# An expert stage in 16 units of several blocks, with TensorE in written order and weights in 8 KB pairs

## The chip, the cores and the metric

The kernel runs on one core of a Trainium2 chip. The core has five engines that work side by side, each through its own list of instructions in order: TensorE (PE, matrix products; its weight loads are PEld), VectorE (DVE), ScalarE (ACT), GpSimd (POOL) and SyncE (SP). SP here only issues loads. Sixteen DMA engines move data between the chip's memory (HBM) and the on-chip memory (SBUF); TensorE writes its products into PSUM banks of 128 x 512 floats. The metric is the time of one launch in microseconds, the median of several runs.

## What is computed

One decoder block for 512 tokens of width 1024: a mixer (a Mamba-2 part and a short convolution), then a mixture of experts, each with a residual and a layer norm. The change concerns the mixture:

```python
def moe_ffn(h, router_w, router_bias, w_gate, w_up, w_down, sh_gate, sh_up, sh_down):
    ...
    _, e_idx = lax.top_k(jnp.where(expert_mask, biased, -jnp.inf), TOP_K)
    gate = jnp.take_along_axis(scores, e_idx, axis=1)
    gate = gate / jnp.sum(gate, axis=-1, keepdims=True) * ROUTED_SCALE
    ...
    def expert_block(args):
        xb, e = args
        return (jax.nn.silu(xb @ w_gate[e]) * (xb @ w_up[e])) @ w_down[e]
    ...
    routed = jax.ops.segment_sum(yb * row_gate[:, None], row_tok, num_segments=T + 1)[:T]
    shared = (jax.nn.silu(hf @ sh_gate) * (hf @ sh_up)) @ sh_down
    return (routed + shared).reshape(b, s, d)
```

There are 64 experts; each token goes to 8 of them. An expert has a gate and an up matrix of 1024 x 256 and a down matrix of 256 x 1024, 3.1 MB in float32. So 201 MB of weights are read by whatever tokens there are. All arithmetic is in float32.

## The kernel before

The first 800 us or so are the mixer, then come the output projection, the routing and the shared expert. The expert stage begins at 872 us. Two experts have their place fixed at build time (the "static" unit); the other 62 are ranked by their number of tokens, and the ranks are read into registers, so that each load takes its expert from a register.

**Blocks.** A block is 128 slots of tokens, gathered from memory by an indirect DMA on POOL (`slots`, line 1055). There are 41. In 13 of them all slots belong to one expert: these use `matmul3` (lines 124 to 127), three matmuls for one product, since weights and tokens are split into a high and a low part (`split`: ScalarE writes the high part, line 130, VectorE the rest, line 132). In the other 28 several experts share the block, 64 or 32 slots each: these use `tiled` (line 883), which for one step issues a matmul per expert, each on its own columns of the array, with unsplit float32 weights. A step is one of the 8 slices of 128 of the contraction in the up part, or one of 2 x 2 in the down part, so a tiled block has 12.

**Units.** `kinds` makes the units by letter: x is the heaviest expert with its partner (three blocks), y and z a heavy expert with a lighter one (a plain and a tiled block), f one full expert, a, p and q tiled blocks of two, two and four experts. `ORDER` has 31 letters; with the static unit that is 32 units. Every unit runs through `ffn` in stages: quarters 0 to 3 of gate and up, activation (`act_t`, with transposes), then down, whose results `expert` scales (line 1083) and splits. After every second finished block (`GRP`) `combine` puts rows back in token order by 16 matmuls for each block (lines 1106, 1107) and eight adds on VectorE (line 1112). The first quarter of the next unit is written ahead of this unit's down part. A scheduler orders every engine's instructions by when they can run, TensorE's too.

**Weights.** `piece` loads a quarter of gate and up (two DMAs of 256 KB, rows of 2 KB) or half of down (one of 512 KB, rows of 4 KB) into a page of 4 KB in each of the 128 partitions: ten DMAs for each expert. Pages come from a pool of 14 (`pages`), which the mixer uses too, and some from a second pool (`pb_`). `plan` writes down the loads in order, `take` issues them up to `AHEAD` pieces before they are used. All go through SP's one queue, and a load waits there until its page is free.

Of the kernel before, what the change touches and what calls it, by code (L numbers as in the profile page):

```python
# [26 lines left out]
NPAGB = 9  # L27
# [5 lines left out]
XA = 3  # L33
# [3 lines left out]
ORDER = "azqxqyyppaypayaaafazaaafafafpaz"  # L37
AHEAD = 14
# [3 lines left out]
BEY = 100  # L42
# [11 lines left out]
PSPLIT = (3,)  # L54
NPS = 0
SPB = ((0, 0, 0), (0, 1, 0), (0, 0, 1), (0, 1, 1), (0, 0, 2))
# [7 lines left out]
def block_kernel(ctx: ExitStack, tc: tile.TileContext, a, out, dbg=None):  # L64
# [9 lines left out]
    pa = ctx.enter_context(tc.tile_pool(name="pages", bufs=NPAGE))  # L74
# [15 lines left out]

    def page(shape, dt=F32, pool=None):
        n = 1
        for q in shape:
            n *= q
        assert n == 1024
        return (pool or pa).tile([P, *shape], dt, name="pg", tag="pg")
# [39 lines left out]
    def split(src, eng=None):  # L136
# [8 lines left out]
        elif len(src.shape) == 4:  # L145

            split_to(hi, lo, src.rearrange("p a b c -> p (a b c)"), eng)
            return tuple(t.rearrange("p (a b c) -> p a b c", a=src.shape[1], b=src.shape[2]) for t in (hi, lo))
# [134 lines left out]
    for k in range(KD):  # L283
        if k + 1 < KD:
            ada_mm(k + 1)
        for i, c0 in enumerate(first):
            if k == 0:
                if i < 3:
                    fw[i] = split(win.pop(c0))
                else:  # L290
                    fw[i] = (page([KD, P], FR), page([KD, P], FR))
# [76 lines left out]
    def ssd_proj(g):  # L368
        d = sst.setdefault(g, {})
        if g == 0:  # L370
# [3 lines left out]
            parts_ = page([KD, P], FR), page([KD, P], FR)  # L374
# [32 lines left out]
    def ssd_core(g):  # L407
# [97 lines left out]
        for i in range(2):  # L505
            tl = 2 * g + i
            if tl % 2 == 0:
                d0 = (page([2, T], FR), page([2, T], FR))
# [29 lines left out]
    def sc_conv(j):  # L538
# [18 lines left out]
        if j % 2 == 0:  # L557
            d0 = (page([2, T], FR), page([2, T], FR))
# [162 lines left out]
    sgb = [page([2, T]) for _ in range(4)]  # L721
# [21 lines left out]
    def wo_load():  # L743
# [3 lines left out]
        if j < 5:  # L747
            pool = pb_ if j < 2 else pa
            wo.append((page([D], FR, pool), page([D], FR, pool)))
# [87 lines left out]
    def piece(q, wg, wu, wd, pool=None):  # L837

        if q < 4:
# [8 lines left out]
    def xsplit(src_ap, dst=None, whole=False):  # L848
# [4 lines left out]
        for q in range(2):  # L853
            tp = bank("tr", 2)
            for k in range(4):
                transpose(tp[:, k * P:(k + 1) * P], sv[:, 4 * q + k, :])
            tv = tp.rearrange("p (k n) -> p k n", k=4)
            sl_ = slice(4 * q, 4 * q + 4)
            if whole:
                S.activation(hi[:, sl_, :], tv, AF.Copy)  # L860
            else:
                split_to(hi[:, sl_, :], lo[:, sl_, :], tv)
        return hi, lo

    def act_t(o, whole):
# [3 lines left out]
        V.tensor_tensor(sg, sg, o[:, FE:], op=OP.mult)  # L869
        tp = bank("tr", 2)  # L870
# [375 lines left out]
    for i, u in enumerate(units):  # L1246
        steps += [(u, j) for j in (1, 2, 3)]
        if i + 1 < len(units):
            steps.append((units[i + 1], 0))
# [176 lines left out]
```

## Time and profile before

| what | us |
|---|---|
| median of three runs | 1611.98 (1609.96 to 1613.97) |
| the profiled execution | 1601.06 |
| its span | 1599.3 |
| expert stage in it, first tiled matmul to last combine matmul | 712.2 (872.3 to 1584.5) |

The profile is one execution. Its time is 1.8 us more than its span. Everything below is read from this execution; the runs that were timed lie some 10 us above it. Lines of the trace name an operation by its source line, the tile it writes and the tiles it reads: `ps_pj<-pg,xt` is a product of a weight page and transposed tokens into a PSUM bank. `xN` counts records.

### The profile page before, as it was taken

What the parts mean: (1) busy time and instruction counts of PE and PEld (TensorE: products, weight loads), DVE (VectorE), ACT (ScalarE), POOL (GpSimd) and SP (SyncE); (2) the same over time, 40 slices, a digit from 0 to 9 for tenths busy, and PEclk for the clock granted to TensorE, in tenths of its full rate; (3) what the DMA queues carried; (4) which work ended last, traced back from release to release, by engine and by line L of the source; (5) the groups of instructions that cost most, each with busy time, mean ns of one, the idle gap of its engine ahead of it and who ended that gap; (6) DMA issues with size and microseconds to landing.
All of it is one profiled execution on the core that took longest, in us unless ns stands there. A gap on an engine that the chain in (4) does not pass through costs nothing. (4 is left out here: it accounts for less than half of the span.)

```text
span 1599.3 us, 24806 instructions
## 1 busy us (share of the span) xinstructions
PE 1525.1 (95%) x8253; PEld 1009.2 (63%) x8253; DVE 978.3 (61%) x1760; ACT 643.3 (40%) x926; POOL 312.5 (20%) x314
## 2 busy tenths in 40 slices
PE   6999899999999999999988899999999999999996
PEld 4688787787787877888765445454454445446643
DVE  5557778667868656536786354564464456447646
ACT  3556575555634545434441323142233123223323
POOL 0011111011001456400035121221111212111211
PEclk9999999999999999999989999999999999999998
DMA  9763333534340677626363989787999799899991
GB/s 277 178 166 94 101 78 80 147 84 101 105 116 17 195 222 223 174 79 199 151 211 100 289 280 367 268 311 212 343 322 315 247 365 334 245 333 328 360 316 66
DMA packets 240599, 335.82 MB, mean 210 GB/s; under 512 B 18548, under 2 KB 141780, under 8 KB 240468
## 3 DMA queue, kind: packets, MB, share of 16 engines
q1 hardware_dynamic: 229380, 303.75, 59.3%
q0 software_dynamic: 11088, 30.45, 7.0%
q8 instruction: 67, 1.10, 0.3%
q14 instruction: 64, 0.52, 0.1%
HBM read 334.58 MB, written 4.28 MB: 212 GB/s over the span
## 5 line engine op out<-in xcount | busy, mean ns | idle before, releaser
L132 DVE TENSOR_TENSOR wl<-pg,wh 128x1024 fp32r<-128x1024 f32 (+1 forms) x201 | 245.5, 1226 | 164.2 <-ACT wh L130 163.8
L130 ACT ACTIVATE wh<-pg 128x1024 fp32r<-128x1024 f32 (+1 forms) x207 | 202.2, 987 | 232.5 <-PE ps_pj L126 101.9
L125 PE MATMUL ps_pj<-hm,wh 128*128 128x512 f32 x680 | 274.6, 405 | 2.1 <-ACT wh L130 2.1
L127 PE MATMUL ps_pj<-hm,wl 128*128 128x512 f32 x680 | 267.0, 393 | 5.5 <-DVE wl L132 5.5
L126 PE MATMUL ps_pj<-hm,wh 128*128 128x512 f32 x680 | 266.4, 392 | 0.0
L887 PE MATMUL ps_pj<-pg,xt 128*32 128x512 f32 (+1 forms) x1472 | 247.7, 600 | 0.0
L125 PEld LDWEIGHTS ps_pj<-hm,wh 128*128 128x128 f32 x680 | 128.1, 188 | 36.2 <-issue 5.5
L127 PEld LDWEIGHTS ps_pj<-hm,wl 128*128 128x128 f32 x680 | 128.0, 188 | 35.5 <-DVE wl L132 8.3
L126 PEld LDWEIGHTS ps_pj<-hm,wh 128*128 128x128 f32 x680 | 128.0, 188 | 28.8 <-issue 3.4
L887 PEld LDWEIGHTS ps_pj<-pg,xt 128*32 128x32 f32 (+1 forms) x1472 | 63.4, 115 | 110.8 <-issue 101.8
L1112 DVE TENSOR_TENSOR res<-res,ps_y 128x512 f32<-128x512 f32 x152 | 102.6, 686 | 42.1 <-PE ps_y L1107 40.4
L1083 DVE SCALAR_TENSOR_TENSOR wk<-ps_y,red,pg 128x512 f32<-128x512 f32 x82 | 61.1, 748 | 88.1 <-PE ps_y L887 57.1
L1055 POOL DMA_INDIRECT pg<-h_d,idx x41 | 49.8, 1215 | 326.7 <-DVE oh L1039 78.5
L887 PE MATMUL ps_y<-pg,wkr 128*32 128x512 f32 (+1 forms) x736 | 107.5, 596 | 2.0 <-DMA pg<-in_w_down_dram 2.0
L1079 POOL TENSOR_SCALAR oht<-iota_t,tok 128x512 fp32r<-128x512 f32 x41 | 67.1, 1642 | 129.1 <-PE ps_y L1107 128.9
L1107 PE MATMUL ps_y<-pg,oht 128*128 128x512 f32 x224 | 89.4, 402 | 0.0
L338 POOL TENSOR_TENSOR pg<-pg 128x1024 f32<-128x1024 f32 x28 | 73.9, 2653 | 53.9 <-ACT pg L336 53.8
L868 ACT ACTIVATE sg<-ps_pj 128x256 f32<-128x256 f32 x44 | 16.9, 384 | 163.9 <-PE ps_pj L887 112.2
L122 PEld LDWEIGHTS ps_tr<-ident,pg 128*128 128x128 f32 x392 | 56.7, 191 | 34.4 <-ACT wkr L878 10.8
L125 PE MATMUL ps_pj<-pg,wh 128*128 128x512 f32 x192 | 75.0, 391 | 2.8 <-ACT zs L403 2.8
L127 PE MATMUL ps_pj<-pg,wl 128*128 128x512 f32 x192 | 75.3, 392 | 0.0
L122 PE MATMUL ps_tr<-ident,pg 128*128 128x128 f32 x392 | 68.6, 290 | 6.8 <-DMA pg<-h_d,idx 1.8
(383 smaller groups left out, 2550.9 us busy)
## 6 DMA issues: line engine op xcount, KB each, us to landing
pg<-in_w_gate_dram SPq DMA_DIRECT2D x256, 256.0 KB
pg<-in_w_up_dram SPq DMA_DIRECT2D x256, 256.0 KB
pg<-in_w_down_dram SPq DMA_DIRECT2D x128, 512.0 KB
pg<-in_w_in_dram SPq DMA_DIRECT2D x88, 512.0 KB
pg<-in_w_ada_dram SPq DMA_DIRECT2D x48, 512.0 KB
bc<-acs_d POOLq DMA_DIRECT2D x32, 256.0 KB, 5.2
pg<-in_w_ssd_out_dram SPq DMA_DIRECT2D x16, 512.0 KB
pg<-in_w_sc_out_dram SPq DMA_DIRECT2D x8, 512.0 KB
```

The costliest lines, as they stand in the source:

```text
L122: return PE.transpose(o, i, ident[:n, :n])
L125: PE.matmul(o, lh, rh, start=start, stop=False)
L126: PE.matmul(o, lh, rl, start=False, stop=False)
L127: PE.matmul(o, ll, rh, start=False, stop=stop)
L130: S.activation(hi, src, AF.Copy)
L132: V.tensor_tensor(lo, src, rw(hi), op=OP.subtract)
L338: GP.tensor_tensor(part[i], part[i], w, op=OP.add)
L887: PE.matmul(o[w * i:w * i + w, :], x[:, w * i:w * i + w], m, start=start, stop=stop, tile_position=(0, w * i))
L1079: GP.tensor_scalar(res_[b][0], iota_t, tok, None, op0=OP.is_equal)
L1083: V.scalar_tensor_tensor(yg, o, red[:, 1:2], g2b[:, ns_], op0=OP.mult, op1=OP.mult)
L1107: PE.matmul(o, oh_, yl[:, ns_], start=False, stop=(i == len(parts) - 1))
L1112: V.tensor_tensor(ra[t][:, ns_], ra[t][:, ns_], o, op=OP.add)
```

## The change

- **Units.** 32 units become 16: the static one, and 15 words of letters. The blocks of all letters of a word form one unit, so that a unit has one to three blocks and two to six experts.
- **Order in a unit.** All its blocks go through quarter 0, then through quarter 1 in reverse order, and so on. Then follow the activations with two steps or more of the combine of the unit before between them, the transposes of the next unit's tokens, and the down part. `csteps` takes all finished blocks of the unit before at once, up to three where it was two before.
- **TensorE in written order.** From the second unit on, TensorE's instructions stand as the program writes them (`tc.manual_schedule`); the other engines are still ordered by the scheduler.
- **Memory.** The pool of single pages ends after the shared expert's loads; a pool of seven pairs of 8 KB is opened in its place, taken in the fixed order `PORD`. One more pair comes from `pb_` for every eighth piece, so eight pairs rotate.
- **Loads.** A piece is half of gate and up (two DMAs of 512 KB, rows of 4 KB) or the whole of down (one of 1 MB, rows of 8 KB): five DMAs for each expert. `AHEAD` is 10 pieces.
- **The count of overflowing tokens** (`beyond`) is cut in three steps and put between others.

```diff
--- before.py
+++ after.py
@@ -24,22 +24,25 @@
 NPAGE = 14
-NPAGB = 9
+NPAIR = 7
+
+PORD = (4, 6, 3, 5, 1, 0, 2)
+NPAGB = 5
+NPAPB = 2
...
 GRP = 2
-XA = 3
+MAN = 1
 NXG = 3
...
-ORDER = "azqxqyyppaypayaaafazaaafafafpaz"
-AHEAD = 14
+ORDER = "x qy ya ap za qff ya ap za faa ya ap za faa p"
+AHEAD = 10
...
@@ -71,7 +71,9 @@
-    pa = ctx.enter_context(tc.tile_pool(name="pages", bufs=NPAGE))
+
+    pa_cm = tc.tile_pool(name="pages", bufs=NPAGE, side="right")
+    pa, pw = pa_cm.__enter__(), []
@@ -88,12 +90,38 @@
+    def pair(shape, dt=F32, pool=None):
...
+        if pool:
+            return pool.tile([P, *shape], dt, name="pr", tag="pr", bufs=NPAPB)
+        npr[0] += 1
+        return pw[0].tile([P, *shape], dt, name="pr", tag="pr%d" % PORD[npr[0] % NPAIR])
...
@@ -836,37 +863,73 @@
     def piece(q, wg, wu, wd, pool=None):
 
+        if q < 2:
+            r = pair([2, 4, FE], pool=pool)
+            for i, w in enumerate((wg, wu)):
+                SY.dma_start(r[:, i], w.rearrange("(p k) n -> p k n", k=KD)[:, 4 * q:4 * q + 4, :])
+        else:
+            r = pair([2, D], pool=pool)
+            SY.dma_start(r, wd.rearrange("(p k) n -> p k n", k=2))
+        return r
...
         if q < 4:
-            r = page([2, 2, FE], pool=pool)
+            r = page([2, 2, FE])
             for i, w in enumerate((wg, wu)):
                 SY.dma_start(r[:, i], w.rearrange("(p k) n -> p k n", k=KD)[:, 2 * q:2 * q + 2, :])
         else:
-            r = page([D], pool=pool)
+            r = page([D])
             SY.dma_start(r, wd.rearrange("(p k) n -> p k n", k=2)[:, q - 4, :])
         return r
...
@@ -887,27 +950,33 @@
-            for o, (xh, xl), b in zip(os_, xs, blocks):
+            for o, (xh, xl), b in list(zip(os_, xs, blocks))[::-1 if q % 2 else 1]:
                 for k in (2 * q, 2 * q + 1):
...
             if q == 3:
-                acts = [act_t(o, len(b) > 1) for o, b in zip(os_, blocks)]
+                sgs = [act_in(o) for o in os_]
             yield
+        acts = []
+        for sg, b in zip(sgs, blocks):
+            acts.append(act_t(sg, len(b) > 1))
+            yield
+        yield
...
@@ -1087,30 +1161,34 @@
             if n == 1:
                 parts.append(res_[b])
-                if len(parts) == GRP and not tail[0]:
-                    combine()
...
-    def combine(last=False):
-
+    def csteps(last=False):
+
+        ps_ = list(parts)
+        parts.clear()
         for t in range(NT):
...
@@ -1131,8 +1209,13 @@
-    shw = [piece(q, a["sh_gate"][0], a["sh_up"][0], a["sh_down"][0]) for q in range(6)]
-    ring = [lambda: (page([D], FR, pb_), page([D], FR, pb_)),
+    shw = [page_piece(q, a["sh_gate"][0], a["sh_up"][0], a["sh_down"][0]) for q in range(6)]
+    pa_cm.__exit__(None, None, None)
+    pw.append(ctx.enter_context(tc.tile_pool(name="pairs", bufs=1, side="right", reuse_waits="tile")))
+    for i in range(NPAIR):
+
+        pw[0].tile([P, 2048], F32, name="pl", tag="pr%d" % i)
+    ring = [lambda: two([D], FR, pb_),
             lambda: (rww.rearrange("p k i e -> p (k i e)"), page([D], FR, pb_)), lambda: (hm[6], hm[7])]
...
@@ -1239,39 +1321,44 @@
-    units += [kinds[k].pop(0) for k in ORDER.replace(" ", "")]
+    for ks in ORDER.split():
+
+        rs, bl = (), []
+        for k in ks:
+            r_, b_ = kinds[k].pop(0)
+            bl += [(tuple(len(rs) + e for e in es), sl_) for es, sl_ in b_]
+            rs += r_
+        units.append((rs, bl))
...
@@ -1303,25 +1392,42 @@
+    def unit(n):
...
+        need_x(i1)
+        run = expert([b for b, _ in units[n][1]], sl[i0:i1], xs[i0:i1], lambda e, q: take((n, e, q), AHEAD))
+        for _ in range(4):
+            next(run)
+        com = csteps() if parts else iter(())
+        for _ in range(2):
+            next(com, None)
+        for _ in range(i1 - i0):
+            next(run)
+            next(com, None)
+        zipper(xs_steps(i2), com, islice(over_, 1))
+        next(run)
+        tail[0] = n + 1 == len(units)
+        drain(run)
...
-    running, i1 = {}, 0
-    for i, (u, j) in enumerate(steps):
-        if j == 0:
-            i0 = ublk[id(u)]
-            i1 = i0 + len(u[1])
-            need_x(i1)
-            running[id(u)] = expert([b for b, _ in u[1]], sl[i0:i1], xs[i0:i1],
-                                    lambda e, q, n=unum[id(u)]: take((n, e, q), AHEAD),
-                                    PSPLIT if unum[id(u)] < NPS else ())
-        if i + XA < len(steps) and steps[i + XA][1] == 0 and len(xs) == i1:
-            need_x(i1 + 1)
...
-        next(running[id(u)], None)
-    combine(True)
+    for n in range(MAN):
+        unit(n)
+    over_ = beyond()
+
+    with tc.manual_schedule(engines={mybir.EngineType.PE}):
+        for n in range(MAN, len(units)):
+            unit(n)
+        combine(True)
+    ostart, oend, obase, nov = far
```

Three things are the same: the number of TensorE instructions, that of gathers, and the order of TensorE, VectorE and ScalarE up to the expert stage. VectorE has 32 fewer adds.

TensorE before, in a unit with one plain and one tiled block of two experts, first and second quarter (L887 is a tiled matmul, L125 to L127 are the three of `matmul3`, `ps_pj` the banks of the up part, `pg` a weight page):

```order
L125 MATMUL ps_pj<-wh_80,xt 128x512
L126 MATMUL ps_pj<-wl_81,xt 128x512
L127 MATMUL ps_pj<-wh_80,xt 128x512
L887 MATMUL ps_pj<-pg,xt 64x512 x3
L125 MATMUL ps_pj<-wh_76,xt 128x512
L887 MATMUL ps_pj<-pg,xt 64x512
L126 MATMUL ps_pj<-wl_77,xt 128x512
L127 MATMUL ps_pj<-wh_76,xt 128x512
```

Of the four tiled matmuls that make two steps, three stand together and the fourth is apart, behind a plain one: the second step is cut.

TensorE after, in a unit with a plain block, a tiled block of two experts and one of four (`ya`; lines moved: L950 is `tiled`, L153 to L155 `matmul3`, `pr` a pair), from the end of the down part before it to the second quarter:

```order
L950 MATMUL ps_y<-pr,wkr 64x512 x8
L153 MATMUL ps_pj<-wh_76,xt 128x512
L154 MATMUL ps_pj<-wl_77,xt 128x512
L155 MATMUL ps_pj<-wh_76,xt 128x512
L153 MATMUL ps_pj<-wh_76,xt 128x512
L154 MATMUL ps_pj<-wl_77,xt 128x512
L155 MATMUL ps_pj<-wh_76,xt 128x512
L950 MATMUL ps_pj<-pr,xt 64x512 x4
L950 MATMUL ps_pj<-pr,xt 32x512 x16
L950 MATMUL ps_pj<-pr,xt 64x512 x4
L153 MATMUL ps_pj<-wh_78,xt 128x512
```

The tiled blocks of quarter 0 and quarter 1 stand in one row, 4 + 16 + 4 matmuls, with nothing between them, and the plain block's matmuls stand ahead and behind.

SP before, loads of gate and up pages and of down pages (a register and an ISA row ahead of each load fetch the expert's number):

```order
L842 DMA pg<-in_w_up_dram 128x512
L842 REGISTER_ALU
L842 ISA
L842 DMA pg<-in_w_gate_dram 128x512
L842 REGISTER_ALU
L842 ISA
L842 DMA pg<-in_w_up_dram 128x512
L845 REGISTER_ALU x2
L845 ISA
L845 DMA pg<-in_w_down_dram 128x1024
L845 REGISTER_ALU x2
L845 ISA
```

SP after, at the same kind of place:

```order
L869 DMA pr<-in_w_up_dram 128x1024
L869 REGISTER_ALU x2
L869 ISA
L869 DMA pr<-in_w_gate_dram 128x1024
L869 REGISTER_ALU x2
L869 ISA
L869 DMA pr<-in_w_up_dram 128x1024
L872 REGISTER_ALU x2
L872 ISA
L872 DMA pr<-in_w_down_dram 128x2048
L872 REGISTER_ALU x2
L872 ISA
```

Where there was a load of 128 x 512 floats for a quarter and 128 x 1024 for half of down, there is now one of 128 x 1024 for a half of gate or up and one of 128 x 2048 for the whole of down.

## Rows read from the trace of the kernel before

**Rows 1.** The head of the page

```profile
span 1599.3 us, 24806 instructions
```

**Rows 2.** Windows, the expert stage: us, busy us (instructions) per engine, clock, DMA share, GB/s

```profile
872.30:1584.50 712.20, 696.40 (x4152) 354.15 (x4150) 379.83 (x648) 205.47 (x328) 131.86 (x123) 1.00 0.87 295
```

**Rows 3.** Waits of TensorE in the stage: us, times, longest

```profile
PE ps_y L1106 <- ACT rww L130: 2.7, 2, 2.2
```

**Rows 4.** Groups by form in the stage: shapes xcount, busy us, mean ns, idle before

```profile
L887 PE MATMUL ps_pj<-pg,xt 128*32 128x512 f32 x1152 | 156.7, 597 | 0.0
L1112 DVE TENSOR_TENSOR res<-res,ps_y 128x512 f32<-128x512 f32 x152 | 102.6, 686 | 42.1 <-PE ps_y L1107 40.4 <-issue 1.1
L887 PE MATMUL ps_pj<-pg,xt 128*64 128x512 f32 x320 | 91.3, 612 | 0.0
...
L132 DVE TENSOR_TENSOR wl<-pg,wh 128x1024 fp32r<-128x1024 f32 x72 | 88.5, 1233 | 51.1 <-ACT wh L130 51.0
L130 ACT ACTIVATE wh<-pg 128x1024 fp32r<-128x1024 f32 x72 | 75.0, 1054 | 102.6 <-DMA pg<-in_w_up_dram 41.9 <-DMA pg<-in_w_down_dram 27.7 <-PE ps_pj L127 22.9
L887 PE MATMUL ps_y<-pg,wkr 128*32 128x512 f32 x576 | 71.0, 596 | 2.0 <-DMA pg<-in_w_down_dram 2.0
...
L887 PE MATMUL ps_y<-pg,wkr 128*64 128x512 f32 x160 | 36.5, 598 | 0.0
```

**Rows 5.** Timeline of TensorE: start, us, line, out<-in, xcount

```profile
999.51 1.05 PE L887 MATMUL ps_pj<-pg,xt 128*32 128x512 f32 x2
1000.48 0.50 PE L1106 MATMUL ps_y<-rww,oht 128*128 128x512 f32 x1
...
1002.30 1.05 PE L887 MATMUL ps_pj<-pg,xt 128*32 128x512 f32 x2
1003.27 0.50 PE L1107 MATMUL ps_y<-hm,oht 128*128 128x512 f32 x1
```

**Rows 6.** Timeline of TensorE, two other places

```profile
1014.61 3.65 PE L887 MATMUL ps_y<-pg,wkr 128*64 128x512 f32 x16
1018.20 0.50 PE L1106 MATMUL ps_y<-pg,oht 128*128 128x512 f32 x1
...
1330.74 1.06 PE L887 MATMUL ps_pj<-pg,xt 128*32 128x512 f32 x8
1331.74 0.51 PE L1107 MATMUL ps_y<-pg,oht 128*128 128x512 f32 x1
1332.08 0.39 PE L1106 MATMUL ps_y<-pg,oht 128*128 128x512 f32 x1
1332.32 0.39 PE L1107 MATMUL ps_y<-pg,oht 128*128 128x512 f32 x1
```

**Rows 7.** DMA queue in 6 us (961, 1027, 937, 973): packets, MB, share

```profile
q1 hardware_dynamic: 627, 2.27, 99.5%
...
q1 hardware_dynamic: 683, 2.49, 102.2%
...
q1 hardware_dynamic: 1072, 1.95, 98.7%
...
q1 hardware_dynamic: 1163, 2.12, 101.9%
```

**Rows 8.** DMA issues in the stage: count, median us to landing

```profile
pg<-h_d,idx POOLq DMA_INDIRECT x40, 8.2
```

**Rows 9.** Waits of SP's queue, 880 to 1560: us, times, longest

```profile
SPq L842 <- PE ps_pj L887: 65.2, 32, 9.4
...
SPq L845 <- PE ps_y L887: 40.7, 18, 12.0
```

**Rows 10.** Timeline of TensorE, and a window's row at the clock's fall

```profile
882.60 1.18 PE L122 MATMUL ps_tr<-ident,pg 128*128 128x128 f32 x8 [1.85 <-DMA pg<-h_d,idx]
883.72 5.39 PE L887 MATMUL ps_pj<-pg,xt 128*64 128x512 f32 x16
...
883.70:887.10 3.40, 3.40 (x7) 0.76 (x6) 0.00 (x0) 0.73 (x2) 0.21 (x1) 0.51 0.83 301
```

More of the change, by code (lines that the diff above doesn't have):

```diff
@@ L41 @@
 NADA = 3
-BEY = 100
 ENG3 = ("PP", "VV", "VV", "VV")
@@ L95, in page, with two @@
         assert n == 1024
-        return (pool or pa).tile([P, *shape], dt, name="pg", tag="pg")
+        if pool or not pw:
+            return (pool or pa).tile([P, *shape], dt, name="pg", tag="pg")
+        if not halves:
+            t = pair([2, 1024], dt)
+            halves.extend((t[:, 1], t[:, 0]))
+        return halves.pop()
+    def two(shape, dt=F32, pool=None):
+        if pool:
+            t = pair([2, *shape], dt, pool)
+            return t[:, 0], t[:, 1]
+        return page(shape, dt), page(shape, dt)
     def wk():
@@ L557, in sc_conv @@
         if j % 2 == 0:
-            d0 = (page([2, T], FR), page([2, T], FR))
+            d0 = two([2, T], FR)
             for q in range(2):
@@ L718, in block_kernel @@
         next(ada, None)
-    sgb = [page([2, T]) for _ in range(4)]
+    sgb = [h for _ in range(2) for h in two([2, T])]
     for j in range(KD):
@@ L747, in wo_load @@
         if j < 5:
-            pool = pb_ if j < 2 else pa
-            wo.append((page([D], FR, pool), page([D], FR, pool)))
+            wo.append(two([D], FR, pb_ if j < 2 else None))
             split_to(*wo[j], r)
@@ L852, in xsplit, with steps, act_in @@
         sv = src_ap.rearrange("p (d k) -> p k d", k=KD)
[L853 to L865, printed above, removed]
+        def steps():
+            for q in range(2):
+                tp = bank("tr", 2)
+                for k in range(4):
+                    transpose(tp[:, k * P:(k + 1) * P], sv[:, 4 * q + k, :])
+                tv = tp.rearrange("p (k n) -> p k n", k=4)
+                sl_ = slice(4 * q, 4 * q + 4)
+                if whole:
+                    S.activation(hi[:, sl_, :], tv, AF.Copy)
+                else:
+                    split_to(hi[:, sl_, :], lo[:, sl_, :], tv)
+                yield
+        return (hi, lo), steps()
+    def xsplit(src_ap, dst=None, whole=False):
+        r, g = xsteps(src_ap, dst, whole)
+        for _ in g:
+            pass
+        return r
+    def act_in(o):
         sg = rt.tile([P, FE], F32, name="sg", bufs=2)
@@ L1058, in slots, with expert_piece, expert @@
         return xg, red
-    def expert_piece(sel_, q, pool=None):
-        return piece(q, *(a[nm][0, sel_].rearrange("o d f -> (o d) f") for nm in ("w_gate", "w_up", "w_down")), pool)
+    npc = [0]
+    def expert_piece(sel_, q):
+        npc[0] += 1
+        return piece(q, *(a[nm][0, sel_].rearrange("o d f -> (o d) f") for nm in ("w_gate", "w_up", "w_down")),
+                     None if npc[0] % (NPAIR + 1) != 3 else pb_)
     npart, tail = [0], [False]
-    def expert(blocks, sl_, xs, w, gp=()):
+    def expert(blocks, sl_, xs, w):
         res_ = []
@@ L1112, in combine @@
                     V.tensor_tensor(ra[t][:, ns_], ra[t][:, ns_], o, op=OP.add)
-        parts.clear()
+                yield
+    def combine(last=False):
+        for _ in csteps(last):
+            pass
     out_proj(0)
```

97 lines of the change are left out of this document (56 added, 41 removed).

## The prediction, made before the change was run

> **What bounds the kernel now.** I read the head of the page first [rows 1], then the busy time by stretch [rows 2], TensorE's waits [rows 3] and the instruction groups of the expert stage [rows 4]. The change touches nothing before the first tiled matmul (872.3 us) but the order of some loads, so only the stage from there to the last combine matmul (1584.5 us) matters: 712.2 us of the 1599.3 us span. In it TensorE is busy 696.4 us, the DMA engines 87% [rows 2]. TensorE is idle only 15.8 us there, and the list of what its matmuls waited for has nothing above 2.7 us [rows 3]. VectorE and ScalarE work half the time or less. So what would shorten the stage is less TensorE time, and DMA is the next thing in line: 0.87 x 712 = 620 us busy.
>
> But not all TensorE time is matrix work. Two prices show it.
> - A **run of tiled matmuls** (line 887) costs more than its steps. One step of a block (all its tiles, 8 records for four tiles) between two combine matmuls holds TensorE from 1330.74 to 1331.74, 1.00 us; the plain matmul behind it takes 0.34 instead of the 0.23 of its neighbours. Four steps in one run last 1014.61 to 1018.20, 3.59 us [rows 6]. With about 0.1 us lost at each end, one step and its ends are 1.20 us, four are 3.79; the difference gives 0.86 us a step and about 0.34 us for each run.
> - A **step that is cut** pays again. Two records of a four-tile step, a quarter of it, take 0.97 us before the next kind of matmul, and so does the next quarter [rows 5]: the four tiles work side by side, so a piece takes as long as the whole. Each cut costs another 0.86 us.
>
> 28 of the 41 blocks are tiled, 12 steps each, 336 steps: 289 us. The four L887 groups of TensorE add up to 156.7 + 91.3 + 71.0 + 36.5 = 355.5 us [rows 4], 66 us more. The scheduler that orders TensorE by readiness makes 133 tiled runs out of them with 42 extra passes for cut steps (counted in the order of instructions, of which two places stand above): 133 x 0.34 = 45 and 42 x 0.86 = 36 us. That is 81 us; records overlap and some fall on waits, so the agreement is rough but the excess is there.
>
> **What the change removes.** TensorE in program order from the second unit on, with the blocks of a unit reversed on odd quarters so that tiled blocks meet: 47 runs and 3 extra passes. Saved: 86 x 0.34 = 29 us and 39 x 0.86 = 33.5 us, **62.5 us** on the path. The number of matmuls is the same. 32 fewer adds on VectorE (152 x 686 ns before, [rows 4]) save 22 us of an engine that doesn't bound: nothing.
>
> **What it changes in the loads.** Rows of 2 KB for gate and up become 4 KB, of 4 KB for down 8 KB; a quarter of an expert's ten DMAs becomes half of five. Before has both sizes side by side: in 6 us stretches with only 4 KB rows the DMA queue moves 2.27 MB at 99.5% of the engines' time and 2.49 at 102.2%, so 380 and 406 GB/s; with only 2 KB rows 1.95 MB at 98.7% and 2.12 at 101.9%, 329 and 347 GB/s [rows 7]. A pair of 1.05 MB is then 2.76 us at 380, and 3.10 at 338 if size doesn't matter. I take 2.76, as the first is the row with the new size. With 64 x 3 pairs and 41 gathers (0.52 MB each, so 1.4 us at the same rate) the loads need 530 + 57 = 587 us, against 620 now. Issuing is off the path: SP mostly waits for buffers, 65.2 us for one reader alone [rows 9].
>
> The Trainium skill ("DMA: Bandwidth & Descriptors", Specifications) puts the HBM limit of one core at about 358 GB/s, which speaks against a gain from longer rows. By it a pair would take an estimated 2.93 us and the loads 620 us. The trace passes that limit at 380 and 406 GB/s [rows 7], so I stay with the measured rate.
>
> **What it adds: waits.** Eight pairs rotate (seven of the pool and one of the hold), in fixed order, and a pair is read by all blocks of a unit, so that a unit's first-half pairs come free only when TensorE has done its first two quarters. Piece j waits for the release of piece j-8, at the head of SP's queue, with all later loads behind it.
> - Units of six experts (qy, qff): two of six second-half pairs are there, four must come after the release: 1.1 us to start and 4 x 2.76 = 12.1 us. TensorE has one tiled block's two steps (1.7 us) and a plain block's six matmuls (1.4 us) to do in between: 9 us idle, twice, 18 us.
> - Units of five (faa, twice): two must come, 6.6 us less 3.1 us: 3.5 us, twice, 7 us.
> - Units of four fit in eight pairs. The three ap have two blocks for four experts, less TensorE than DMA work, and pay about 1 us each, one more for the others: 4 us.
> - The start: unit 0 is loaded ahead, unit x waits for gathers that land 8.2 us after issue [rows 8] with nothing else in TensorE's fixed order, 8 us. Before, other units' matmuls slipped in.
> - In the five units with late or just-landed halves, a plain block also waits for its split, 1.05 us on ScalarE and 1.23 on VectorE [rows 4], now in sequence with landing: 5 x 2.3 = 11 us.
> - The clock: after the wait of 1.85 us at 882.6 the next 16 records take 5.39 us instead of the 3.65 of the same 16 at 1014.61 [rows 6, 10], at a granted clock of 0.51 over 3.4 us [rows 10], which is the 1.2 GHz level. 1.74 us for each long idle time; four of them, 7 us.
> - The tail: the last combine has only one block's 16 matmuls, 3.7 us, under 8 adds of 686 ns, 5.5 us; with a split ahead of it, 4 us.
>
> Sum 59 us. Against it go the waits of before, which have other causes and fall away: at least the 15.8 us idle, some 20 with the half clock that follows them. Net 39 us added. The bounds: nothing added if the ring never runs dry (0), and 78 us if every unit of four pays what a unit of five does (11 x 3.5 = 39 more).
>
> **The sum.** 712.2 - 62.5 + 39 = 688.7 us for the stage, 23.5 us less. The profiled execution took 1601.06 us, so it would be 1577.5; the median of the runs is 1611.98, 0.7% above it, and the same 23.5 us off gives **1588.5 us**. As its own range I give 1572 to 1604 (waits of 20 us more or less).
>
> **Rivals.**
> 1. **The ring keeps up.** If the tiled runs are saved and waits stay what they are now, 712.2 - 62.5 = 649.7 us: 1549.5. For it: DMA needs 587 us of 650, and some units (ya, za) have slack that the next could use. Against it: eight 1 MB pairs are only 22 us of loads, and a six-expert unit needs twelve before its up part ends.
> 2. **Longer rows bring nothing.** At 3.10 us a pair, units of six take 60 us of loads against 45 of TensorE work, those of five 51 against 45, ap 41 against 35. Adding the larger of the two for each of the 16 units gives about 677 us; with start, splits, clock and tail (30 us) 707 us, 5 us under now: 1607. For it: single 2 KB stretches reach 347 GB/s, not far from 380, and the stage as a whole moves 295 GB/s at 0.87 share, 339 when busy [rows 2]. Against it: the four stretches of rows 7 order themselves by row size.
> 3. **Slower: the queue head.** SP works in order, so a pair that waits for release holds every later load, also the next unit's first half. If the units of four pay for this as the units of five do, 3.5 us each in 11 units, waits are 98 us instead of 59: 712.2 - 62.5 + 78 = 727.7, 15.5 us more: 1627.5. It decides once the added waits pass 62.5 us. For it: TensorE in fixed order can't do anything else meanwhile, and the trace has SP waiting for a TensorE reader up to 12.0 us at a time already [rows 9]. Against it: the arithmetic of four experts gives eight pairs for eight slots, and downs go out while quarters three and four run.
>
> **How the numbers follow.** 0.3% of this time, about 5 us, is about what a measurement of this kernel can tell from no change. Forecast 0.52, rival 1 0.18, rival 2 0.16 (a third of it beyond 0.3% faster, the rest within), rival 3 0.14. Faster: 0.52 + 0.18 + 0.05 = 0.75; same 0.11; slower 0.14. The range reaches from rival 1 to where rival 3 begins to bite: 1550 to 1618, which leaves half of rival 1's low side and most of rival 3 outside.
>
> **What would show it.** The sum of the tiled groups should fall from 355.5 to about 300 us; if it stays, the 62.5 us are wrong. The waits of TensorE should name the gate, up and down loads, some 9 us long in the two six-expert units and 3 to 4 in the five-expert ones; if units of four show them too, it is rival 3. 6 us stretches of the full queue should show 380 GB/s or more; at 340 it is rival 2. The time up to 872 us should be unchanged within 2 us. A TensorE that idles behind VectorE (the split, the add of a combine) more than behind DMA would be a cause that I have not priced.

## The result: 1691 us instead of 1611, and the profile after

The changed kernel takes 1691.12 us (median of 4 runs, 1687.24 to 1693.0) against 1610.97 us of the kernel before on the same chip (4 runs): a ratio of 1.0494, 95% interval 1.0466 to 1.0522. It is 80 us slower, where 23.5 us faster were forecast.

The page of the changed kernel, its head, TensorE's row and the clock and DMA slices:

```profile
span 1691.2 us, 22909 instructions
...
PE 1527.4 (90%) x8253; PEld 1024.9 (61%) x8253; DVE 962.3 (57%) x1728; ACT 642.4 (38%) x925; POOL 315.9 (19%) x314
...
PEclk9999999999999999999898879998799989999997
DMA  9663434425315576253537478776688769787671
```

Compared with [rows 1], 92 us are added to the span of the profiled execution. They lie as follows: the expert stage has 80.6 us more (876.1 to 1668.9, 792.8 us instead of the 712.2 of [rows 2]), the end behind its last combine matmul 7.5 more (22.3 instead of 14.8), and 3.8 us are added ahead of the stage. One trace of the kernel before can't tell the last from variation between executions: the stage begins anywhere from 878.8 to 884.1 us in the kernels below, which share the code of the changed kernel up to there. So stages are compared by length.

The stage in the view of windows (us; busy us of TensorE, its weight loads, VectorE, ScalarE, POOL; granted clock; DMA share; GB/s), to be read against [rows 2]:

```profile
876.10:1668.90 792.80, 692.55 (x4151) 368.53 (x4150) 356.21 (x608) 199.93 (x319) 131.49 (x122) 0.92 0.72 266
```

Two numbers tell most. TensorE is busy 692.55 of 792.8 us, so **idle 100.2 us** where it was idle 15.8; and its granted clock is 0.92 in the mean where it was 1.00. The trace has sixteen stretches at 0.5 (the 1.2 GHz level), 126 us together, against two with 6.8 us before. In 91 of the 126 us TensorE was busy, at half speed, so 45.5 us of them are lost (3.4 before). Busy time less that loss, the work at full clock, is 647.0 us against 693.0 before. The balance: work -46.0, idle +84.4, clock +42.1, sum +80.5 us.

What TensorE's matmuls waited for in the stage (us, times, longest), beside [rows 3]:

```profile
PE ps_tr L150 <- DMA pg<-h_d,idx: 60.2, 11, 8.2
PE ps_pj L950 <- DMA pr<-in_w_up_dram: 25.4, 14, 6.5
PE ps_pj L153 <- ACT wh L158: 3.8, 4, 2.3
PE ps_pj L154 <- DVE wl L160: 2.6, 5, 0.8
```

The gathers of token rows are the largest wait, 60.2 us in eleven waits of up to 8.2 us. Eleven is the number of units with three blocks ahead of which a unit runs (x, qy, ya, za, qff, ya, za, faa, ya, za, faa). The loads of gate and up, which the prediction made the main thing, come second with 25.4.

How one of the eleven arises, at the end of unit qy. First TensorE, then VectorE, then POOL, each as a timeline (start, us, what, idle before it and who ended it):

```profile
1001.54 0.26 PE L1116 MATMUL ps_st<-pay,oh 128*32 128x6 bf16 x16
...
1003.69 0.61 PE L150 MATMUL ps_tr<-ident,pg 128*128 128x128 f32 x4
1004.23 0.26 PE L1116 MATMUL ps_st<-pay,oh 128*32 128x6 bf16 x16
1011.32 1.94 PE L150 MATMUL ps_tr<-ident,pg 128*128 128x128 f32 x8 [6.83 <-DMA pg<-h_d,idx]
```

```profile
1002.25 0.16 DVE L1119 TENSOR_REDUCE red<-ps_st 128x2 f32<-128x6 f32 x1
...
1002.92 0.15 DVE L1121 TENSOR_SCALAR idx<-red 128x1 int32<-128x1 f32 x1
```

```profile
1003.03 2.63 POOL L1153 TENSOR_SCALAR oht<-iota_t,tok 128x512 fp32r<-128x512 f32 x1 [57.22 <-PE ps_y L1181]
1005.82 1.14 POOL L1124 DMA_INDIRECT pg<-h_d,idx  x1 [0.16 <-issue]
```

TensorE computes the slots of a block at 1001.54 (L1116), VectorE has the row numbers at 1002.92, but POOL has just come to a one-hot tile (`oht`, L1153), which waited 57.22 us for the combine's end, and issues the gather only at 1005.82. It lands at about 1011.2. TensorE has gone on from 1003.69 to the next slots and then stands at the transposes of that block from 1004.5 to 1011.32. Nothing else may go ahead of them, for its order is written. Why the slots and the transposes of one block lie only 3 us apart there is in the code. `xs_steps` ends each block `i` with `need_s(i + NXG)`: that writes slots up to block i+2, though the buffer that block i has just left is free for block i+3. In a unit of three blocks the third block's slots therefore come behind the transposes of the first, a few instructions ahead of its own transposes.

The clock right there, in the view of windows:

```profile
1007.10:1017.30 10.20, 5.98 (x36) 2.86 (x40) 2.22 (x6) 2.14 (x3) 5.71 (x7) 0.50 0.43 129
1191.40:1208.50 17.10, 12.28 (x26) 4.99 (x27) 4.72 (x4) 4.00 (x4) 0.00 (x0) 0.50 0.88 324
```

It falls to 0.50 from 1007.1 on, in the middle of the wait, and stays there for 10.2 us; 17.1 us at 1191.4, where TensorE was waiting for loads.

The tiled groups, to be read against [rows 4]:

```profile
L950 PE MATMUL ps_pj<-pr,xt 128*32 128x512 f32 x1152 | 145.8, 604 | 18.3 <-DMA pr<-in_w_up_dram 18.3
...
L950 PE MATMUL ps_pj<-pr,xt 128*64 128x512 f32 x320 | 82.0, 626 | 7.7 <-DMA pr<-in_w_up_dram 7.1 <-issue 0.6
...
L950 PE MATMUL ps_y<-pr,wkr 128*32 128x512 f32 x576 | 72.4, 651 | 0.8 <-DVE wk L1157 0.8
...
L950 PE MATMUL ps_y<-pr,wkr 128*64 128x512 f32 x160 | 39.7, 617 | 0.0
```

They sum to 339.9 us where they summed to 355.5. The prediction said about 300. 37 us of these records lie in the stretches at 0.5; at full clock the groups would take some 321 us.

And SP's queue, against [rows 9]:

```profile
SPq L869 <- PE ps_y L950: 260.3, 25, 24.8
SPq L869 <- PE ps_pj L950: 137.2, 17, 21.5
```

SP waits 260 us for pairs that the down part of a unit holds. The loads don't lack time: the stage moves 266 GB/s at a share of 0.72, 369 when busy, where it was 339. They lack buffers, and these lack TensorE.

### The profile page after: what moved, and what is told of

It is laid out like the page before. It is cut to its first block, busy times and chain, and to the rows that moved or that the text cites. A ratio compares the mean times of both kernels' runs of the same rounds, so it can differ in the third digit from the quotient of the medians.

```text
span 1691.2 us, 22909 instructions
## 1 busy us (share of the span) xinstructions
PE 1527.4 (90%) x8253; PEld 1024.9 (61%) x8253; DVE 962.3 (57%) x1728; ACT 642.4 (38%) x925; POOL 315.9 (19%) x314
## 4 chain that ended last, share of the span: by engine, by line
PE 68%; DMA 13%; DVE 7%; issue 6%; ACT 3%; POOL 2%; SPq 1%; DVEq 0%; POOLq 0%; ACTq 0%
PE ps_pj L153 12%; PE ps_pj L154 11%; PE ps_pj L155 11%; PE ps_pj L950 8%; DMA pr<-in_w_up_dram 6%; PE ps_y L950 5%; PE ps_tr L150 4%; PE ps_y L1180 4%; PE ps_y L1181 4%; DMA pg<-h_d,idx 4%; DMA pg<-in_w_ada_dram 2%; PE ps_y L153 1%; DVE wl L160 1%; PE ps_y L483 1%; POOL pg L366 1%
## 5 line engine op out<-in xcount | busy, mean ns | idle before, releaser
L153 PE MATMUL ps_pj<-hm,wh 128*128 128x512 f32 x680 | 274.9, 405 | 1.6 <-ACT wh L158 1.6
L155 PE MATMUL ps_pj<-hm,wl 128*128 128x512 f32 x680 | 266.7, 393 | 5.3 <-DVE wl L160 5.3
L950 PE MATMUL ps_pj<-pr,xt 128*32 128x512 f32 (+1 forms) x1472 | 226.4, 609 | 26.1 <-DMA pr<-in_w_up_dram 25.4
L160 DVE TENSOR_TENSOR wl<-pg,wh 128x1024 fp32r<-128x1024 f32 (+1 forms) x129 | 159.3, 1241 | 112.7 <-ACT wh L158 112.4
L160 DVE TENSOR_TENSOR wl<-pr,wh 128x1024 fp32r<-128x1024 f32 x72 | 85.9, 1221 | 163.2 <-ACT wh L158 163.2
L158 ACT ACTIVATE wh<-pg 128x1024 fp32r<-128x1024 f32 (+1 forms) x135 | 127.5, 952 | 132.2 <-PE ps_pj L154 98.9
L950 PEld LDWEIGHTS ps_pj<-pr,xt 128*32 128x32 f32 (+1 forms) x1472 | 61.8, 117 | 173.0 <-issue 167.4
L1153 POOL TENSOR_SCALAR oht<-iota_t,tok 128x512 fp32r<-128x512 f32 x41 | 76.9, 1879 | 472.6 <-PE ps_y L1181 470.5
L153 PEld LDWEIGHTS ps_pj<-hm,wh 128*128 128x128 f32 x680 | 128.0, 188 | 35.9 <-issue 6.6
L155 PEld LDWEIGHTS ps_pj<-hm,wl 128*128 128x128 f32 x680 | 127.9, 188 | 34.7 <-DVE wl L160 7.0
L158 ACT ACTIVATE wh<-pr 128x1024 fp32r<-128x1024 f32 x72 | 73.3, 1051 | 180.0 <-DMA pr<-in_w_down_dram 80.8
L150 PE MATMUL ps_tr<-ident,pg 128*128 128x128 f32 x392 | 72.2, 318 | 64.1 <-DMA pg<-h_d,idx 60.2
L1186 DVE TENSOR_TENSOR res<-res,ps_y 128x512 f32<-128x512 f32 x120 | 82.2, 686 | 56.2 <-PE ps_y L1181 55.0
L950 PE MATMUL ps_y<-pr,wkr 128*32 128x512 f32 (+1 forms) x736 | 111.8, 643 | 0.8 <-DVE wk L1157 0.8
L153 PE MATMUL ps_pj<-pg,wh 128*128 128x512 f32 x192 | 75.9, 395 | 1.1 <-ACT zs L431 1.1
L155 PE MATMUL ps_pj<-pg,wl 128*128 128x512 f32 x192 | 76.2, 397 | 0.0
```

Of the source, the lines that this page charges most:

```text
L150: return PE.transpose(o, i, ident[:n, :n])
L153: PE.matmul(o, lh, rh, start=start, stop=False)
L155: PE.matmul(o, ll, rh, start=False, stop=stop)
L158: S.activation(hi, src, AF.Copy)
L160: V.tensor_tensor(lo, src, rw(hi), op=OP.subtract)
L950: PE.matmul(o[w * i:w * i + w, :], x[:, w * i:w * i + w], m, start=start, stop=stop, tile_position=(0, w * i))
```

## The experiments

All are edits of the changed kernel; gather3_five and the kernels from mid on hold the edit of gather3 too, and those from mid on that of mid. "Work" is TensorE's busy time in the stage with half of what lies at the lower clock taken off; "half" is the time in the stage at the 1.2 GHz level.

| kernel | median us | stage | idle | half | work |
|---|---|---|---|---|---|
| before | 1610.97 | 712.2 | 15.8 | 7 | 693 |
| changed | 1691.12 | 792.8 | 100.2 | 126 | 647 |
| gather3 | 1631.34 | 727.6 | 55.7 | 48 | 654 |
| gather3_five | 1620.73 | 714.1 | 47.9 | 38 | 651 |
| sched (one run) | 1646.84 | 739.3 | 48.0 | 41 | 675 |
| oht_dve (one run) | 1678.00 | 769.9 | 87.2 | 89 | 646 |
| fill (one run) | 1678.25 | 775.4 | 55.5 | 68 | 693 |
| mid | 1619.38 | 713.3 | 47.8 | 43 | 645 |
| mid_tail | 1609.72 | 714.3 | 49.5 | 48 | 646 |
| mid_five | 1593.79 | 693.8 | 37.8 | 21 | 648 |
| mid_five_rows | 1594.44 | 701.6 | 40.0 | 31 | 647 |
| mid_five_sched | 1606.77 | 709.7 | 20.3 | 17 | 683 |
| cuts | 1617.18 | 717.5 | 34.3 | 27 | 673 |

The kernel before gave medians of 1608.9 to 1613.1 us beside them.

**gather3: the gathers a block earlier.**

```diff
-            need_s(i + NXG)
+            need_s(i + 1 + NXG)
```

> The changed kernel with one number changed: the slots and the gather of a block are written three blocks ahead of its transposes instead of two, so that the third gather of a three-block unit is issued a unit earlier. Theory A (TensorE, in written order, reaches the transposes of each unit's third block just after it has done the slots for that very gather, and idles through issue and landing; the idle time then lowers the clock): TensorE's waits for gathers fall from 60.2 us to under 15, time at the half clock from 126 us to under 60, the time from 1691 to 1600-1630 us. Rival B (gathers are late because POOL has the one-hot tiles, which wait for the combine, ahead of them): gather waits fall by a third at most, 1665-1685 us. Rival C (the ring of eight pairs is the bound, gather waits only cover it): gather waits go, waits for gate and up loads grow by as much, 1670-1691 us.

Measured: 1631.34 us, 1.0119 of the kernel before (1.0074 to 1.0164), so 60 us of the 80 are gone with one number. TensorE's waits in its stage:

```profile
PE ps_pj L950 <- DMA pr<-in_w_up_dram: 27.2, 17, 5.2
PE ps_tr L150 <- DMA pg<-h_d,idx: 6.5, 1, 6.5
```

One gather wait of eleven is left (the first, for unit x, which has only the one block of the static unit ahead of it), and the half clock falls from 126 to 48 us. The waits for loads stay where they were, so rival C falls. Theory A holds; the time is just over the upper end of its range.

**oht_dve: nothing but gathers on POOL.** The lines that make the index and the one-hot tile:

```diff
-                GP.tensor_scalar(tok, red[:, 0:1], NOTOK, None, op0=OP.add)
-                GP.tensor_scalar(res_[b][0], iota_t, tok, None, op0=OP.is_equal)
+                V.tensor_scalar(tok, red[:, 0:1], NOTOK, None, op0=OP.add)
+                V.tensor_scalar(res_[b][0], iota_t, tok, None, op0=OP.is_equal)
```

> The changed kernel with the one-hot tiles and their index made on VectorE instead of POOL, so that nothing but gathers stands in POOL's queue there. Theory A: the gather of the third block is still written too late; waits for gathers stay above 45 us of 60, time 1675-1695 us. Rival B (POOL's queue holds the gathers): they fall under 25 us, time 1620-1650 us.

```profile
PE ps_tr L150 <- DMA pg<-h_d,idx: 46.3, 10, 6.6
```

46.3 us instead of 60.2, 1678.00 us in one run. So POOL's queue was 14 us of the gather waits, the place in TensorE's order the rest. Theory A again, with a share for B.

**fill: work in the wait.** Ahead of the transposes of a unit's third block, in ten units, with `NFILL` = 5 (the added products are read by nobody; the lines that choose the units are left out):

```diff
+            if fill and i == n - 1 and i >= 3:
+                o = bank("tr", 2)
+                for j in range(NFILL):
+                    PE.matmul(o, ident, g2b[:, :512], start=(j == 0), stop=(j == NFILL - 1))
```

> The changed kernel with 43 us of idle matrix work added: in ten of the eleven units that wait for a gather, five float32 products of 128 x 512 (0.86 us each) into a bank nobody reads stand on TensorE just ahead of the transposes that wait. Theory: the clock falls because TensorE idles there; with work in the wait, the time at the half clock falls from 126 us to under 70, and the time from 1691 to 1655-1678 us although work is added. Rival (the clock falls for another reason): half clock stays above 110 us and the time is 1690-1705 us.

```profile
878.80:1654.20 775.40, 719.87 (x4251) 377.90 (x4250) 356.90 (x608) 199.25 (x319) 132.89 (x122) 0.96 0.73 272
```

46 us more work, 45 us less idle time, and the half clock falls from 126 to 68 us; 1678.25 us in one run, 13 us less than without the added work, just outside the expected range on the slow side. The rival (another reason for the clock) falls: with TensorE kept busy through the waits nearly half of the lower clock is gone. So of the changed kernel's loss a part, here 19 us, is a price for waiting that no list of waits shows.

**sched: the scheduler's order again.**

```diff
-MAN = 1
+MAN = 16
```

(and the steps of `beyond` are made ready ahead of the first unit).

> The changed kernel with TensorE ordered by the scheduler in all units, as before the change; units, pairs and loads stay. Its order has 78 tiled runs and 43 passes for cut steps instead of 47 and 3. By the prediction's prices (0.34 us a run, 0.86 a cut) the tiled groups take 45 us more TensorE time. Theory A: the scheduler puts other work into the gather waits, so idle time of TensorE falls from 100 us to 40-60 us and the half clock with it; 1640-1690 us. Rival D (the written order has nothing to do with the waits): idle time stays at 100 us and the time rises to about 1735 us.

```profile
883.50:1622.80 739.30, 691.29 (x4151) 360.82 (x4150) 355.57 (x608) 199.32 (x319) 128.75 (x121) 0.97 0.77 286
```

1646.84 us in one run: 44 us faster than the changed kernel, 53.5 us in the stage. Idle falls to 48 us, work rises from 647 to 674.5. So the written order did save TensorE work, 27.5 us of it, and cost 52 us of idle time and some 29 us of clock. The range for the time was right, the price of the order (45 us) was not.

```profile
PE ps_tr L150 <- DMA pg<-h_d,idx: 29.6, 11, 6.9
PE ps_pj L950 <- DMA pr<-in_w_up_dram: 4.6, 6, 1.5
```

The waits for gathers fall from 60.2 to 29.6 us and those for loads from 25.4 to 4.6. So the scheduler finds other work for half of the gather waits, but all eleven are still there: the program still writes the slots two blocks ahead.

This run also splits the 46 us. Between before and sched the cuts are nearly equal in number (42 and 43 extra passes), and there are 55 fewer runs: 18.5 us of work, 0.34 us each, if the runs are all that makes the difference. That is the price of the prediction.

**gather3_five: no unit of six experts.**

```diff
-ORDER = "x qy ya ap za qff ya ap za faa ya ap za faa p"
+ORDER = "x qf ya ap za qf ya ap za faa ya ap za fa ya p"
```

> As gather3, and the words of letters regrouped so that no unit has six experts (qf twice instead of qy and qff; 17 units instead of 16, the same blocks). Theory A with the ring rule of the prediction (a unit of n experts has 2n first and second halves for eight slots, so six pay about 9 us and five 3.5 us each): the waits for gate and up loads, 25.4 us in the changed kernel, fall by 8 to 18 us against gather3, and the time by 10 to 25 us. Rival (loads are late because DMA is slow over all, not for the slots): waits move to other units, within 5 us of gather3.

1620.73 us, 1.0050 (1.0026 to 1.0074) of before, 10.6 us under gather3. The time came out as expected, the reason didn't: waits for loads are 24.8 us instead of 27.2, spread over more units.

```profile
PE ps_pj L950 <- DMA pr<-in_w_up_dram: 24.8, 17, 4.9
```

Seventeen waits of up to 4.9 us. Half of the 24.8 us is in the three units of five (4.8, 5.0 and 2.4 us), nearly all the rest in seven of the ten units of four (0.4 to 3.2 us each), for which the prediction had 4 us in all. Its rule counted slots and forgot time. A unit's second-half pairs take the slots of the unit before's downs, which come free only when its down part is done. In the units ap TensorE reaches the third quarter some 10 us after that, and the last late pair is there 12.0 to 12.8 us after it; in two units ya it is 14 and 17 us against 18 in both.

**mid: the combine between the second and the third quarter.**

```diff
-        for _ in range(4):
+        for _ in range(2):
             next(run)
         com = csteps() if parts else iter(())
-        for _ in range(2):
+        for _ in range(4):
             next(com, None)
+        for _ in range(2):
+            next(run)
+        next(com, None)
```

> gather3 with the combine of the unit before moved from behind the fourth quarter to between the second and the third (four of its eight steps there, one behind the fourth quarter, three between the activations). Reason to test: a unit's second-half pairs are requested only when the down part of the unit before releases its pairs, and land 1.1 + 4 x 2.76 = 12 us later, while TensorE reaches the third quarter about 10 us after that release; 7 to 11 us of combine in between would cover it, in units of four too, which the prediction had called free. If so: waits for gate and up loads fall from 27 us to under 10, waits for splits from 10 to 5, the time from 1631 to 1603-1616 us, with six more tiled runs (2 us) against it. Rival (DMA is late over all): waits move to the down loads or the next unit's first half, time within 8 us of gather3.

1619.38 us (1.0049, 1.0025 to 1.0072), 12 us under gather3, just over the expected range. The waits:

```profile
PE ps_tr L150 <- DVE xt L160: 8.6, 9, 3.3
PE ps_pj L153 <- ACT wh L158: 7.6, 4, 2.7
PE ps_pj L950 <- DMA pr<-in_w_up_dram: 5.3, 3, 2.0
```

The waits for loads fall from 27.2 to 5.3 us, so the reason is right: it was the time between the release and the third quarter. The stage is 14.3 us shorter than that of gather3: 7.9 us of idle time and 9.0 of work, less 2.6 more that the clock takes. Why work falls although six more runs stand in the order is taken up below, with the saving. But the combine had also covered the splits behind it. Transposes now wait 8.6 us for VectorE's part of `xt`, and 7.6 us for ScalarE's splits: a wait took the place of a wait, and idle time falls by 8 us in all where 22 us of waiting for loads are gone.

**mid_tail and mid_five: the end, and the units of six.** mid_tail is mid with p moved from the end to the middle, mid_five also has no unit of six. The units of mid, then those of mid_tail and of mid_five:

```diff
-ORDER = "x qy ya ap za qff ya ap za faa ya ap za faa p"
...
+ORDER = "x qy ya ap za qff ya ap za p faa ya ap za faa"
...
+ORDER = "x qf ya ap za qf ya ap za p faa ya ap za fa ya"
```

> mid with the same words of letters, the unit of one block (p) moved from the end to the middle, so that a unit of three blocks is combined last; the two units of six experts stay. If the one-block end costs what the two traces show (22 us behind the last combine matmul against 14), this gives 7 to 9 us of the 25.6 us between mid and mid_five: 1609 to 1613 us. The other 17 us then belong to the units of six experts. Rival (most of the 25.6 us is the end): 1595 to 1602 us.

> mid with units of at most five experts, and a unit of three blocks at the end instead of one of one block (17 units). After the last combine matmul the changed kernel needed 22.3 us to the end and the kernel before 14.8; with three blocks to combine last, the norms of the first rows lie under its matmuls again: 6 to 8 us less. With the waits of six experts gone as well: 1585 to 1602 us, faster than the kernel before by 0.6 to 1.7%. Rival (the ring still stops the loads): 1605 to 1615 us.

mid_tail: 1609.72 us, 0.9975 (0.9948 to 1.0002). Its stage is as long as mid's (714.3 and 713.3 us), its end 13.9 us instead of 22.3: the end was worth 8.4 us in the trace, 9.7 in the medians. mid_five: **1593.79 us, 0.9895 (0.9867 to 0.9922)**, faster than both kernels. The units without six experts gave the other 16 us (they also make a unit of five into one of three, and add one unit).

```profile
882.30:1576.10 693.80, 655.99 (x4151) 349.97 (x4150) 366.67 (x624) 203.92 (x329) 131.91 (x123) 0.99 0.82 304
```

```profile
PE ps_pj L153 <- ACT wh L158: 9.3, 3, 3.8
...
PE ps_pj L950 <- DMA pr<-in_w_up_dram: 4.0, 3, 1.9
```

The waits for loads are down to 4.0 us, DMA has a share of 0.82. TensorE is still idle 37.8 us; the largest wait named is for the splits of plain blocks. Of the 16 us over mid_tail the loads explain little: its waits for them were 7.1 us. Idle time fell by 11.7 us in all and the loss at the lower clock by 10.7. The size was as expected; what in the new units brought it is not shown.

**mid_five_rows: rows of 2 KB again.**

```diff
             for i, w in enumerate((wg, wu)):
-                SY.dma_start(r[:, i], w.rearrange("(p k) n -> p k n", k=KD)[:, 4 * q:4 * q + 4, :])
+                for h in (0, 2):
+                    SY.dma_start(r[:, i, h:h + 2], w.rearrange("(p k) n -> p k n", k=KD)[:, 4 * q + h:4 * q + h + 2, :])
```

> mid_five with every gate and up load cut in two of 256 KB with rows of 2 KB into the same pair, as the kernel before had them; downs keep rows of 8 KB. If row length sets the rate (329 to 347 GB/s against 380 to 406 in the kernel before): rate over busy time falls by 15 to 30 GB/s, the waits for loads come back in part, 5 to 20 us more than mid_five. If it doesn't: within 4 us of mid_five.

```profile
883.90:1585.50 701.60, 661.61 (x4151) 352.15 (x4150) 367.17 (x624) 204.60 (x329) 131.74 (x123) 0.98 0.85 301
```

1594.44 us against 1593.79: no difference. The rate did move: 301 GB/s at a share of 0.846, 356 when busy, against 304 at 0.823, 370. So with longer rows the traffic is quicker by 4%, and the time doesn't show it. That fits with loads that wait for buffers: SP waits for pairs that TensorE holds 225 us here and 420 us in mid_five, so slower loads use up time in which SP would have waited.

**mid_five_sched and cuts: what the order and a cut are worth.**

```diff
-MAN = 1
+MAN = 17
```

(and the steps of `beyond` are made ready ahead of the first unit).

> mid_five with TensorE ordered by the scheduler instead of as written: 84 tiled runs and 46 extra passes for cut steps against 52 and 2. With few waits in either, this is the price of the order by itself. The prediction's prices give 32 x 0.34 + 44 x 0.86 = 49 us more TensorE time; what the changed kernel and its scheduled form showed (27.5 us for 31 runs and 40 cuts) gives 29 us. Some waits may go, as the scheduler fills them. Expected 1615 to 1640 us, slower than mid_five by 1.3 to 2.9%. Rival (the written order was no gain in the end): within 5 us of mid_five.

```profile
880.90:1590.60 709.70, 689.35 (x4151) 353.57 (x4150) 363.66 (x624) 203.37 (x329) 131.16 (x124) 0.99 0.80 298
```

1606.77 us (0.9974 of before), 13 us slower than mid_five. Work rises by 35 us (648 to 683), idle falls from 37.8 to 20.3. With the gathers in time the written order is worth having, but it still gives half of its 35 us back as waits. The difference is under the expected range: the expectation had named the waits that the scheduler fills, and had put no number on them.

cuts puts 24 cuts into mid_five, by moving a plain block's last matmul into the middle of the tiled step behind it (the lines that hold that matmul back are left out):

```diff
         for i, m in enumerate(ws):
+            if i == len(ws) // 2 and held_mm:
+                held_mm.pop()()
             PE.matmul(o[w * i:w * i + w, :], x[:, w * i:w * i + w], m, start=start, stop=stop,
```

> mid_five with 24 cuts put in by hand: in 24 quarters where a plain block stands ahead of a tiled one, the plain block's last matmul is moved into the middle of the tiled block's first step. That gives 24 more tiled runs and 24 more passes (76 and 26 against 52 and 2), nothing else. By the prices of the prediction, 0.34 us a run and 0.86 a cut, TensorE's work at full clock rises from 648 us by 29 us, and the time to 1615-1623 us. By the price that the pairs with and without the written order gave (35 us for 32 runs and 44 cuts, so about 0.55 a cut) it rises by 21 us, and the time to 1608-1615 us. If a cut costs nothing of its own, 8 us.

```profile
884.10:1601.60 717.50, 683.19 (x4151) 354.05 (x4150) 367.16 (x624) 204.36 (x329) 133.42 (x123) 0.98 0.80 294
```

1617.18 us, 23.4 more than mid_five, and 24.8 us more work (672.8 to 648.0): 1.03 us for a cut with its run, between the 0.88 and the 1.20 that were expected of it. The time lies in the range of the higher price.

## Why the prediction was wrong, step by step

- **What bounds.** TensorE bounds, and its work can be cut by grouping tiled blocks: right. mid_five shows that an expert stage of 694 us exists with 45 us less work than before.
- **The saving, 62.5 us: right in kind, too large.** 46.0 us were measured. The price of a run held (0.34 us, as far as before and sched show it). The cuts were miscounted and priced too high. They were counted in the order of instructions, but a load that comes late cuts a tiled step too, as here in the last unit of five (faa) of the changed kernel:

```profile
1606.93 1.06 PE L950 MATMUL ps_pj<-pr,xt 128*32 128x512 f32 x6 [0.68 <-DMA pr<-in_w_up_dram]
1609.53 2.78 PE L950 MATMUL ps_pj<-pr,xt 128*32 128x512 f32 x24 [1.54 <-DMA pr<-in_w_up_dram]
```

Six of a step's eight records run, then TensorE waits 1.54 us for the pair of the expert that is left. In the changed kernel 11 of the 14 waits for loads stand inside a step like this, in gather3 14, in mid and mid_five 3 each. So the changed kernel ran 14 extra passes and not 3, and a late load costs more than the idle time that its wait shows. The 11 passes between gather3 and mid are some 7 us of the 9 by which mid's work is less, and six more runs stand 2 us against it; the rest is not explained. What is left of 46.0 us for 28 cuts is 17 us, 0.6 each; mid_five and mid_five_sched, with 42 cuts between them counted like this, give 0.57, cuts made by hand 0.69. The work of a stage is not known to better than some 5 us: gather3 has the order of the changed kernel but for its slots, three more such cuts, and 6.9 us more work. So these prices are good to 0.2 us at best. The 0.86 was read from pieces that stand alone [rows 5]. Why a cut costs less than such a piece is not settled.

- **The waits for gathers: the step that failed.** The term "the start", 8 us, priced one unit's wait of this kind (it came as 8.2 us) and put the other ten at nothing. 60.2 us came instead. The instructions' order was counted for runs and cuts but not read for the distance between a gather's slots and its transposes, and [rows 8] had a price ready: a landing of 8 us (4.7 us in the median of the changed kernel, whose eleven waits are 5.5 us in the mean). gather3 proves the step: with that distance one block longer the waits are 6.5 us and the time 60 us less.
- **The clock, 7 us: too small.** 45.5 us are lost at the lower level. The price per wait (1.74 us, [rows 10]) was read from a wait of 1.85 us, after which the clock was low for 3.4 us. With the ten waits of 4 to 8 us in the changed kernel it is low for 6.8 to 17.1 us each. And there were not four such stretches but sixteen.
- **The ring, 29 us: near in the sum, 25.4 us, but not in its parts.** The units of six paid 7.9 and 5.8 us where 9 each was forecast, those of five 1.3 and 2.2 where 3.5 each, and the three units ap 1.6 to 2.7 each where about 1, for the reason that mid showed. That the sum fits is in part luck. **The splits, 11 us:** 6.4.
- **The tail, 4 us: too small.** 7.5 us, behind the last combine matmul; by mid_tail 8 to 10.
- **The loads.** 369 GB/s when busy, against the 380 that was taken and the 338 of rival 2. Of the 6 us stretches of the stage, laid end to end, those with a full queue (a share of 0.97 to 1.05) move 395 GB/s over busy time in the median, where it was 358 before. Right, and without weight: mid_five_rows. The Trainium skill ("DMA: Bandwidth & Descriptors", Specifications) has about 358 GB/s as the HBM limit of one core. Single stretches pass it, as in [rows 7]; the stage as a whole moves 266 GB/s, and only its rate over busy time is above.
- **The rivals.** Slower it was, but not by rival 3. Its sign did show, waits for loads in units of four, but at 2.7 us or less each, and all waits for loads together are under what the forecast had. Its condition was met, added waits of more than 62.5 us: idle time and clock added 126 us net. The mechanism that decided was none of the four. Two of the sums need correcting: there are nine units of four (ya, ap and za, three each) and not eleven, so rival 3 comes to 1620 us instead of 1627.5; and the excesses that rival 2 gives (twice 15, twice 6 and three times 6 us) on 634 us of TensorE work (696.4 - 62.5) make 694 us, not 677.

By terms: the stage was forecast at 688.7 and is 792.8 us, 104 us over. 16.5 us of it are saving that didn't come, 48 are idle time (52 for gathers, less what others stayed under), 38.5 are clock, 1 rounding.

## What to carry to other kernels

An engine whose order is written by hand waits at each instruction whose input is late, so look up, for each input that a slow transfer brings, how far ahead in that same order the instruction stands that starts it; the scheduler had hidden half of what too short a distance costs. Price a wait together with the clock that it takes down, which here made 84 us of added idle time cost 126. And what is moved to cover one wait had covered another: look what stood behind it.

## What the runs showed of the hardware

In these runs the granted clock fell with TensorE's idle time: dead work in the waits took 58 of 126 us at the lower level away and made the kernel 13 us faster (one run), though it had 46 us more to do. A tiled step whose last expert's weights come late pays the wait and also part of another pass: by three comparisons a cut cost 0.57 to 0.69 us of TensorE time. With rows of 4 KB instead of 2 KB for gate and up, beside the same rows of 8 KB for down, the loads of the stage move 370 instead of 356 GB/s of busy DMA time.
